# A hybrid attention layer whose planner is given new tasks: scores and products of a block in one task, weights prepared over nineteen superblocks

## The chip, the cores and the metric

The kernel runs on one core of a Trainium2 chip. The metric is device time in microseconds (us) from start to end of the program. Names of engines: PE is TensorE (matmuls), PEld its weight loads, DVE is VectorE, ACT is ScalarE, POOL is GpSimd, SP is SyncE, which issues most of the transfers.

## What is computed

The reference is one layer of an encoder on two requests (4096 and 2048 tokens of width 1024) with shared weights. Cut to what matters:

```python
hn = rms_norm(x, norm_g); proj = hn @ w_in          # 1024 -> 3072 columns, cut into ten pieces
# A: attention over an 8x16 neighbourhood in a 64-wide token grid, 6 heads
s = q . k + bias + mask;  p = softmax(s);  o = p @ v          (per block of 16 columns, 32 key columns)
ya = neighbourhood(qa, ka, va) * silu(na_g)
# B: windowed attention, blocks of 128 tokens see themselves and both neighbours, 6 q heads, 2 kv heads, sink
yb = windowed(qb, kb, vb, sink) * silu(wg)
# C: attention into 256 memory tokens, 4 heads
yc = memory(qc, km, vm) * silu(mg)
y = concat([ya, yb, yc]) @ w_out;  return x + y
```

Every matmul of the kernel is done with operands split into a high and a low fp16 part, as three products (high x high, high x low, low x high) that are summed in PSUM.

## The kernel before

The tokens are cut into 24 **superblocks** of 256 tokens (16 of one request, 8 of the other), each of two blocks of 128. The program has two **stages**. Stage one does, for each superblock: the x tile is loaded, normed and transposed on PE (`xT`, L527), projected to q, k and v of the neighbourhood heads (L302 to L305, one `proj` task is 24 matmuls of 384 columns), q and k are transposed on PE (L730), the gate is projected (`gaten`, L770 to L772, three tasks of 24 matmuls), and then the neighbourhood attention itself is done. Stage two does the windowed and the memory attention and the output projection (token projection L302 to L305 with 448 columns, gate L1217 to L1219, window scores L1268, window products L1320, memory scores L1348, memory products L1411, output L1491 to L1493).

The neighbourhood attention of a superblock takes three pairs of heads `hp`; for each the four column blocks are taken in two pairs `ab` (`PAIRS = ((1, 2), (0, 3))`). One `qk` task (L930) is one `hp` and one `ab`: 12 matmuls of a 64 x 64 tile into two PSUM banks, one for each head. DVE takes a bank into SBUF with bias and running maximum (L947), ACT does the exponential (L957), ACT and DVE split the result in two fp16 parts (L983, L992), two DMA transposes put it in `pt` (L1003), and a `pv` task (L1019, 24 matmuls inside a request, 16 at its ends) makes the products. The window's `wqk` task is one block and two heads (6 matmuls, two banks, six tasks in a superblock), the memory's `mqk` one block (12 matmuls, two banks), `mpv` one pair of heads.

The eight PSUM banks are slots that tasks hold: `SLOTS = {"pj": [0, 1], "sc": [2, 3, 4, 5], "po": [6, 7]}`. The four `sc` slots serve the scores of all three attentions and, in stage one, the transposes of x and of q and k.

**What sets the order.** No engine's order is written out. Each task is added to a `Plan` with an engine, a duration, a priority, the tasks it depends on and the slots it takes and frees (`acq`, `rel`). `Plan.run` plays the tasks through with these durations: an engine that is free takes the ready task of the lowest priority number whose slots are free, and its instructions are written down at that point. So a duration or a priority in the plan costs nothing on the chip itself, but it moves the static order of each engine. On the chip each engine runs its list in order and waits where a semaphore says so.

**The preparation of stage two's weights.** 24 pieces (8 row blocks of three weight matrices) are each loaded twice while stage one runs: a first pass for the maxima (load L812, DVE), a second for the split (load L812, ACT L844, DVE L849, two stores L858). Their priorities are spread by `step`, whose numerator is `NSB - 12.0`, with NSB = 24. SP issues these loads in one queue with the DMA transposes of the neighbourhood attention.

**The border of the stages.** `w1`, one tile of four parts, holds stage one's split weights (a, b, v and the gate n). When its last reader is done, `f_W` makes `w2` in its place (token weights and a part of the gate's), and the loads `wload` (L1114) follow. `f_T3` closes the pools of stage one and holds one `sc` slot for it.

Of the kernel before, what the change touches and what calls it, by code (L numbers as in the profile page):

```python
# [17 lines left out]
P = 128  # L18
D = 1024
NK = 8  # L20
# [35 lines left out]

class Plan:
# [11 lines left out]
    def add(self, eng, dur, fn, deps=(), prio=0.0, lat=None, acq=(), rel=(), label="", slack=0.0, xf=0.0):  # L69
# [4 lines left out]
        t.dur, t.fn, t.prio = dur, fn, prio + SHIFT.get(label, 0.0)  # L74
# [120 lines left out]
def build(tc, A, out, seqs):  # L195
# [190 lines left out]
    w1 = pools["WS"].tile([P, 4, 2, NK, 384], F16, tag="w", name="w1", bufs=1)  # L386
# [4 lines left out]
    W1 = {"a": w1[:, 0], "b": w1[:, 1], "v": w1[:, 2], "n": w1[:, 3], "m": wm}  # L391
# [246 lines left out]
    for gs_ in range(NSB):  # L638
# [125 lines left out]
        for c in range(3):  # L764
# [8 lines left out]
            prg = gs_ + 0.7 + 0.07 * c  # L773
# [6 lines left out]
            t_t = pl.add("act", 0.45, f_t, [t_g, t_TA, t_hgn], prio=prg - 2, acq=["sgn"], label="tanh")  # L780
# [5 lines left out]
            sgn_done[gs_, c] = pl.add("dve", 0.36, f_sg, [t_t], prio=prg - 2, rel=[("pj", "n", gs_, c)], label="sg")  # L786
        pl.add("free", 0.0, lambda: None, xT_use + last_g, rel=["xT"], label="f")
        w_last = xT_use + last_g
# [11 lines left out]
    step = max(NSB - 12.0, 0.5) / (2 * len(pieces))  # L800
# [72 lines left out]
    for gs_ in range(NSB):  # L873
# [25 lines left out]
        for hp in range(3):  # L899
            t_pvs = []  # L900
            for ab in range(2):
                t_pts = []
# [3 lines left out]
                t_es = []  # L906
                pru = prn + (hp * 4 + ab * 2) / 12.0
# [25 lines left out]
                t_s = pl.add("pe", (3 * nk / 2.4 + 200) / 1000, f_s, base, prio=pru, acq=[("sc", u) for u in us], label="qk")  # L933
                last_qk.append(t_s)
# [73 lines left out]
                def f_pv(gs_=gs_, hp=hp, ab=ab, kgs=kgs, edge=edge):  # L1008
# [14 lines left out]
                t_pv = pl.add("pe", 0.82 * len(kgs) / 3, f_pv, t_pTs + (vdep if ab == 0 else []) + t_pvs[-1:],  # L1023
                              prio=pru, acq=[("po", gs_, hp)] if ab == 0 else [], rel=["pt"], label="pv", slack=0)
                t_pvs.append(t_pv)
                last_pv.append(t_pv)
# [58 lines left out]
    def f_T3():  # L1085

        pl.held["pj", "T3"] = pl.held.pop(("sc", "T3"))
        p_close("YN")
        p_close("YA")
        p_open("YB", "left")  # L1090
        for k in ("wo0", "wo1"):
            one("YB", k, [P, NK, D], F16)
        one("YB", "wtab", [P, 6, 384], F32)
    t_T3 = pl.add("free", 0.0, f_T3, ya_use + [t_TC], acq=[("sc", "T3")], rel=[("pj", "T3")], label="T3")

    def f_W():
        w = pools["WS"].tile([P, 24576], F16, tag="w", name="w2", bufs=1)
        for k, o, n, m in (("wt0", 0, NK, 896), ("wt1", 7168, NK, 896), ("wgb", 18432, 9, 640)):
            st[k] = w[:, o:o + n * m].rearrange("p (k c) -> p k c", k=n)
# [9 lines left out]
    def wload(key, src, dep, pr, n, parts=((0, 4), (4, 8)), o=0, slack=0.0):  # L1109

        ts = []
        for k0, k1 in parts:
            def f(k0=k0, k1=k1):
                SY.dma_start(out=st[key][:, k0 - o:k1 - o, :], in_=src[:, k0:k1, :])  # L1114
            ts.append(pl.add("sp", 0.1, f, [dep], prio=pr, label="w2l", xf=n * (k1 - k0) * 256 / 359e3, slack=slack))
        return ts
    t_wt = wload("wt0", w2_d["t"][0], t_W, Q0 - 3.0, 896) + wload("wt1", w2_d["t"][1], t_W, Q0 - 2.99, 896)
    sg_, so_ = 19.7, 15.0
    t_wg = wload("wgb", w2_d["g"][0], t_W, Q0 - 0.5, 640, slack=sg_) + wload(
        "wgb", w2_d["g"][1], t_W, Q0 - 0.49, 640, ((0, 1),), -8, slack=sg_) + wload(  # L1120
# [113 lines left out]

    for nb in range(NB):
# [3 lines left out]
        kbs = [k for k, ok in ((nb - 1, b > 0), (nb, True), (nb + 1, b < 2 * n - 1)) if ok]  # L1239
# [6 lines left out]
        for jh in range(6):  # L1246
# [4 lines left out]
            if kv == 0:  # L1251
                us = [(nb, j), (nb, 3 + j)]

                def f_s(us=us, kbs=kbs, nb=nb, j=j):

                    runs = []
                    for k in kbs:
                        sl = k % NR2
                        if runs and runs[-1][0] + runs[-1][1] == sl:
                            runs[-1][1] += 1  # L1260
                        else:
                            runs.append([sl, 1])
                    o = 0
                    for r0, nr in runs:
                        for pi, (qv, kk) in enumerate(((0, 0), (0, 1), (1, 0))):
                            for v in range(2):
                                prt = slice(64 * v, 64 * v + 64)
                                T.matmul(bank("sc", "w", us[v])[:, o:o + nr * P], st["qT", nb][prt, 5 * qv + j, :],  # L1268
                                         st["ring2"][prt, kk, r0 * P:(r0 + nr) * P], start=(pi == 0), stop=(pi == 2))
                        o += nr * P  # L1270
                t_s = pl.add("pe", (3 * nk / 2.4 + 220) / 1000, f_s, [k_done[k] for k in kbs] + [q2_done[nb], t_T3], prio=pru,
                             acq=[("sc", "w", u_) for u_ in us], label="wqk")
# [8 lines left out]
            t_t = pl.add("dve", 0.12 + nk * 1.04e-3, f_t, [t_s, t_tab2, t_nsk], prio=pru, acq=["pf2"], rel=[("sc", "w", u)], label="wttr")  # L1281
# [5 lines left out]
            t_e = pl.add("act", 0.46 + nk / 1200, f_e, [t_t], prio=pru, label="wexp")  # L1287
# [10 lines left out]
            t_h = pl.add("dve", 0.13 + nk * 0.53e-3, f_h, [t_r], prio=pru, acq=["phl2"], label="whi")  # L1298
# [302 lines left out]
```

## Time and profile before

| what | value |
|---|---|
| time of the runs, median of 3 | 2679.45 us (2678.18 to 2680.52) |
| the profiled execution: time / span in the trace | 2671.06 us / 2669.0 us |
| PE busy | 2576.2 us, 97% of the span |
| DVE / ACT / POOL busy | 71% / 47% / 20% |
| mean granted TensorE clock | 0.987 |

The page reads so: the first section gives for each engine the time in which it was busy; the second cuts the span in 40 slices of 66.7 us and gives in each the busy share in tenths. A matmul's record lasts longer than the time until the next one starts, since they are pipelined: what a matmul costs is read from start to start.

### The profile page before, as it was taken

How to read it: one execution, taken by the hardware profiler on the slowest of the kernel's cores; microseconds unless marked ns; L12 is line 12 of the kernel's file. 1: busy time of each engine (PE TensorE's matmuls, PEld its weight loads, DVE VectorE, ACT ScalarE, POOL GpSimd, SP SyncE). 2: the span in 40 equal slices, each digit the busy share in tenths (PEclk: the TensorE clock that was granted, in tenths of full speed). 3: DMA queues.
4: the chain of work that ended last, by engine and by line, in shares of the span. 5: the costliest groups of instructions: out<-in, count | busy, mean ns of one | idle time of the engine just before them, and what ended most of it. 6: DMA issues, size and time to landing. Idle time of an engine off the chain costs nothing.

```text
span 2669.0 us, 58144 instructions
## 1 busy us (share of the span) xinstructions
PE 2576.2 (97%) x22056; PEld 1573.0 (59%) x22056; DVE 1886.3 (71%) x5283; ACT 1265.8 (47%) x3553; POOL 528.4 (20%) x690
## 2 busy tenths in 40 slices
PE   6999889999999999899999999999999999999999
PEld 3666656666666666655455555555555555555555
DVE  6476776677676666657987777777777767777775
ACT  7465555666565666544343334334333333333332
POOL 2552223323324433230000000011000100000000
PEclk9999999999999999999999999999999999999999
DMA  5485787668577867697665555555555646565554
GB/s 194 151 179 140 182 194 174 163 163 195 145 171 154 209 154 201 156 194 181 144 140 121 117 133 131 123 120 126 123 121 121 125 109 134 130 132 123 117 116 104
DMA packets 728632, 394.54 MB, mean 148 GB/s; under 512 B 645344, under 2 KB 680960, under 8 KB 727712
## 3 DMA queue, kind: packets, MB, share of 16 engines
q1 hardware_dynamic: 714784, 346.59, 58.7%
q0 software_dynamic: 13568, 44.25, 4.7%
q8 instruction: 172, 2.82, 0.4%
q14 instruction: 108, 0.88, 0.1%
HBM read 153.72 MB, written 80.74 MB: 88 GB/s over the span
## 4 chain that ended last, share of the span: by engine, by line
PE 54%; DVE 3%; DMA 1%; POOL 1%; ACT 0%; issue 0%; SPq 0%; ACTq 0%; DVEq 0%; POOLq 0%
PE bank L1491 6%; PE bank L1492 6%; PE bank L1493 6%; PE bank L302 6%; PE bank L303 5%; PE bank L305 5%; PE bank L1217 4%; PE bank L1219 4%; PE bank L1218 4%; PE bank L1268 3%; PE bank L1320 3%; PE bank L1411 1%; PE bank L1348 1%; POOL r L311 1%; DMA w<-w2dt 0%; DVE phl L1302 0%
## 5 line engine op out<-in xcount | busy, mean ns | idle before, releaser
L302 PE MATMUL bank<-w,xT 128*128 128x384 f16 x1152 | 383.4, 334 | 3.3 <-DVE sc_trow L348 1.9
L303 PE MATMUL bank<-w,xT 128*128 128x384 f16 x1152 | 382.1, 333 | 1.2 <-DVE w L364 1.2
L1285 ACT ACTIVATE pf<-pf,sm 128x384 f32<-128x384 f32 (+1 forms) x288 | 173.0, 601 | 345.6 <-DVE sm L1279 344.5
L1491 PE MATMUL bank<-wo,yT 128*128 128x512 f16 x768 | 291.8, 380 | 0.0
L1492 PE MATMUL bank<-wo,yT 128*128 128x512 f16 x768 | 291.1, 379 | 0.0
L1493 PE MATMUL bank<-wo,yT 128*128 128x512 f16 x768 | 291.1, 379 | 0.0
L309 POOL TENSOR_TENSOR r<-r,wA 128x12 f32<-128x12 f32 x48 | 16.1, 336 | 1288.7 <-DVE r L1170 1260.7
L311 POOL TENSOR_TENSOR r<-r,mhalf 128x12 f32<-128x12 f32 (+1 forms) x100 | 224.9, 2249 | 7.8
L305 PE MATMUL bank<-w,xT 128*128 128x384 f16 x1152 | 210.9, 326 | 0.0
L1279 DVE CUSTOM_DVE_ANT_0 pf<-bank,wtab,nsink 128x384 f32<-128x384 f32 (+1 forms) x288 | 165.3, 600 | 57.9 <-PE bank L1268 57.9
L957 ACT ACTIVATE pf<-pf,sm 128x288 f32<-128x288 f32 (+3 forms) x288 | 156.5, 544 | 81.7 <-DVE sm L947 79.4
L992 DVE SCALAR_TENSOR_TENSOR phl<-pf,sm,phl 128x288 f16<-128x288 f32 (+3 forms) x288 | 151.8, 554 | 47.2 <-ACT phl L983 46.2
L1302 DVE SCALAR_TENSOR_TENSOR phl<-pf,sm,phl 128x384 f16<-128x384 f32 (+1 forms) x288 | 174.5, 606 | 9.1
L983 ACT ACTIVATE phl<-pf,sm 128x288 f16<-128x288 f32 (+3 forms) x288 | 146.7, 544 | 45.0 <-ACT pf L957 21.0
L302 PEld LDWEIGHTS <-xT 128*128 128x128 f16 x1152 | 115.1, 100 | 84.9 <-issue 17.7
L770 PE MATMUL bank<-xT,w 128*128 128x256 f16 x576 | 159.0, 276 | 0.2 <-DVE sc_orow L348 0.2
L771 PE MATMUL bank<-xT,w 128*128 128x256 f16 x576 | 158.6, 275 | 0.0
L303 PEld LDWEIGHTS <-xT 128*128 128x128 f16 x1152 | 114.7, 100 | 74.5 <-issue 9.7
L772 PE MATMUL bank<-xT,w 128*128 128x256 f16 x576 | 158.4, 275 | 0.0
L1297 DVE TENSOR_SCALAR phl<-pf,sm 128x384 f16<-128x384 f32 (+1 forms) x288 | 119.1, 414 | 55.2 <-DMA pt<-phl 37.4
L305 PEld LDWEIGHTS <-xT 128*128 128x128 f16 x1152 | 112.8, 98 | 74.8 <-issue 0.3
L1370 ACT ACTIVATE pf<-bank,smm 128x256 f32<-128x256 f32 x192 | 88.9, 471 | 128.6 <-DVE smm L1364 126.9
(279 smaller groups left out, 6044.9 us busy)
## 6 DMA issues: line engine op xcount, KB each, us to landing
xTd<-xT POOLq DMA_DIRECT2D x48, 512.0 KB, 4.3
out<-xr SPq DMA_DIRECT2D x48, 512.0 KB
xx<-in_x_prompt SPq DMA_DIRECT2D x32, 512.0 KB
xr<-in_x_prompt SPq DMA_DIRECT2D x32, 512.0 KB
x<-xTd SPq DMA_DIRECT2D x24, 512.0 KB
w<-xTd SPq DMA_DIRECT2D x24, 512.0 KB
vd<-vhl POOLq DMA_DIRECT2D x48, 192.0 KB, 3.0
va<-vd SPq DMA_DIRECT2D x48, 192.0 KB
```

Of the source, the lines that this page charges most:

```text
L302: T.matmul(ps, xt[:, kk], wh[:, kk, cols], start=(kk == 0), stop=False)
L303: T.matmul(ps, xt[:, kk], wl[:, kk, cols], start=False, stop=False)
L305: T.matmul(ps, xt[:, NK + kk], wh[:, kk, cols], start=False, stop=(kk == NK - 1))
L311: G.tensor_tensor(out=r, in0=r, in1=mhalf[:, 0:n], op=ALU.pow)
L770: T.matmul(pv, wh, x[:, :, kk, :], start=(kk == 0), stop=False)
L771: T.matmul(pv, wh, x[:, :, NK + kk, :], start=False, stop=False)
L1279: V.tensor_tensor_reduce(out=pf[:, 0:nk], in0=bank("sc", "w", u)[:, 0:nk], in1=st["wtab"][:, h, c0:c0 + nk], scale=-1.0, scalar=nsink[:, h ...
L1285: S.activation(out=pf[:, 0:nk], in_=pf[:, 0:nk], func=AF.Exp, scale=-1.0, bias=sm[:, 0:1], accum_out=sm[:, 1:2])
L1302: V.scalar_tensor_tensor(out=phl[:, nk:2 * nk], in0=st["pfw", u][:, 0:nk], scalar=st["smw", u][:, 3:4], in1=phl[:, 0:nk], op0=ALU.mult, op ...
L1491: T.matmul(ps, yT[:, 0, ts_], st["wo0"][:, c, cs], start=(ci == 0), stop=False)
L1492: T.matmul(ps, yT[:, 0, ts_], st["wo1"][:, c, cs], start=False, stop=False)
L1493: T.matmul(ps, yT[:, 1, ts_], st["wo0"][:, c, cs], start=False, stop=(ci == 7))
```

## The change

It has these parts.

1. **Neighbourhood.** The two `qk` tasks of a pair of heads become one, with 24 matmuls, that takes all four `sc` slots; the two `pv` tasks become one with 48 matmuls that waits for the transposes of both pairs of column blocks and frees two `pt` buffers at its end.
2. **Window.** The six `wqk` tasks of a superblock become three, each with two of the six units (block, pair of heads), four slots; the code is now above the loop over blocks (`win_scores`).
3. **Memory.** The two `mqk` tasks of a superblock become one (four slots); the two `mpv` tasks become one, into two halves of one `po` bank.
4. **Preparation.** `step` goes from `NSB - 12.0` to `NSB - 5.0`: 19 in the place of 12.
5. **The border.** The gate's weights n get a tile of their own (`wn`), so that `w2` follows the last v projection, and the part of stage two's gate weights (`wgb`) the last gate n. `f_T3` holds no slot. The gate tasks of the last two superblocks get a priority 1.0 later. The plan's rate for `wload` goes from 359 to 250 (thousand bytes per us), and a delay (`sg_`) is dropped.
6. **Durations in the plan.** A table `TIMES` overrides the duration of twenty kinds of tasks, almost all of stage two; four formulas of the window's tasks get other constants.

```diff
+TIMES = {"tanh": 0.4, "sg": 0.37, "ev": 0.95, "vl2": 0.235, "red2": 0.9, "r8": 2.85, "nrm2": 1.15, "hi2": 0.89, "lo2": 1.0,
...
-        t.dur, t.fn, t.prio = dur, fn, prio + SHIFT.get(label, 0.0)
+        t.dur, t.fn, t.prio = TIMES.get(label, dur), fn, prio + SHIFT.get(label, 0.0)
...
-    w1 = pools["WS"].tile([P, 4, 2, NK, 384], F16, tag="w", name="w1", bufs=1)
+    w1 = pools["WS"].tile([P, 3, 2, NK, 384], F16, tag="w", name="w1", bufs=1)
+    wn = pools["WS"].tile([P, 2, NK, 384], F16, tag="wn", name="wn", bufs=1)
...
-            prg = gs_ + 0.7 + 0.07 * c
+            prg = gs_ + 0.7 + 0.07 * c + (0.0, 1.0)[gs_ >= NSB - 2]
...
-    step = max(NSB - 12.0, 0.5) / (2 * len(pieces))
+    step = max(NSB - 5.0, 0.5) / (2 * len(pieces))
...
-                t_s = pl.add("pe", (3 * nk / 2.4 + 200) / 1000, f_s, base, prio=pru, acq=[("sc", u) for u in us], label="qk")
-                last_qk.append(t_s)
+                f_ss.append((f_s, nk))
+            t_s = pl.add("pe", sum(3 * nk / 2.4 + 110 for _, nk in f_ss) / 1000, lambda f_ss=f_ss: [f() for f, _ in f_ss], base,
+                         prio=prn + hp / 3.0, acq=[("sc", (gs_, 2 * hp + j, ab)) for ab in range(2) for j in range(2)], label="qk")
+            last_qk.append(t_s)
...
-                t_pv = pl.add("pe", 0.82 * len(kgs) / 3, f_pv, t_pTs + (vdep if ab == 0 else []) + t_pvs[-1:],
-                              prio=pru, acq=[("po", gs_, hp)] if ab == 0 else [], rel=["pt"], label="pv", slack=0)
+            t_pv = pl.add("pe", 1.5 * len(kgs) / 3, lambda f_pvs=f_pvs: [f() for f in f_pvs], pv_deps + vdep,
+                          prio=pru, acq=[("po", gs_, hp)], rel=["pt", "pt"], label="pv")
...
-    t_T3 = pl.add("free", 0.0, f_T3, ya_use + [t_TC], acq=[("sc", "T3")], rel=[("pj", "T3")], label="T3")
+    t_T3 = pl.add("free", 0.0, f_T3, ya_use + [t_TC], label="T3")
...
+    def f_Wn():
+        st["wgb"] = pools["WS"].tile([P, 6144], F16, tag="wn", name="wn2", bufs=1)[:, 0:5760].rearrange("p (k c) -> p k c", k=9)
+    t_Wn = pl.add("free", 0.0, f_Wn, wn_last + prep_done, label="Wn")
...
+        units = [(2 * gs_ + blk, j) for blk in range(2) for j in range(3)]
+        for i in range(3):
+            us = units[2 * i:2 * i + 2]
...
+            t_s = pl.add("pe", sum(3 * len(win_keys(nb)) * P / 2.4 + 80 for nb, _ in us) / 1000, f_s,
...
+                         prio=prw, acq=[("sc", "w", (nb, j + 3 * v)) for nb, j in us for v in range(2)], label="wqk")
...
-            t_s = pl.add("pe", 0.85, f_s, [q2_done[2 * gs_ + blk], t_mk, t_T3], prio=prm + blk / 2.0, acq=[("sc", "m", u) for u in us],
-                         label="mqk")
+        t_s = pl.add("pe", 1.45, f_s, [q2_done[2 * gs_], q2_done[2 * gs_ + 1], t_mk, t_T3], prio=prm,
+                     acq=[("sc", "m", (gs_, hp, blk)) for blk in range(2) for hp in range(2)], label="mqk")
...
-            t_pv = pl.add("pe", 0.82, f_pv, t_pts, prio=prm + hp / 2 + 0.25, acq=[("po", "m", gs_, hp)], rel=["ptm"], label="mpv")
+        t_pv = pl.add("pe", 1.4, f_pv, t_mpts, prio=prm + 0.5, acq=[("po", "m", gs_)], rel=["ptm", "ptm"], label="mpv")
```

What this does to the order of the engines is shown at three places, word for word; a name of a tile ends in the number of its buffer or bank.

PE in the middle of stage two, before: the end of a task of window scores (L1268, two banks) and the output projection (L1491) right behind it.

```order
L1268 LDWEIGHTS qT2_23649
L1268 MATMUL bank5_68<-ring2_16691,qT2_23649 128x384
L1268 LDWEIGHTS qT2_23649
L1268 MATMUL bank2_65<-ring2_16691,qT2_23649 128x384
L1491 LDWEIGHTS yT_22858
L1491 MATMUL bank1_64<-wo0_17780,yT_22858 128x512
```

The same place in the changed kernel, where the first unit of a task ends (window scores are L1273 there):

```order
L1273 LDWEIGHTS qT2_23634
L1273 MATMUL bank3_66<-ring2_16991,qT2_23634 128x384
L1273 LDWEIGHTS qT2_23634
L1273 MATMUL bank2_65<-ring2_16991,qT2_23634 128x384
L1273 LDWEIGHTS qT2_23634
L1273 MATMUL bank4_67<-ring2_16991,qT2_23634 128x384
```

Where a full-size matmul followed the two banks of scores, the scores of two more banks now follow.

DVE in stage two, before: the maxima of the memory scores (L1364), the window's result times its gate (L1465), then the rest of the memory softmax.

```order
L1302 SCALAR_TENSOR_TENSOR phl_25419<-pf_25366,sm_25367,phl_25419 128x384
L1364 TENSOR_REDUCE smm<-bank_68 128x2
L1364 TENSOR_REDUCE smm<-bank_65 128x2
L1465 SCALAR_TENSOR_TENSOR sg<-bank_69,sg 128x128 x3
L1376 TENSOR_SCALAR smm<-smm 128x2
```

And in the changed kernel (the maxima are L1400, L1547 is the last step of an output):

```order
L1547 SCALAR_TENSOR_TENSOR xr<-bank_63,oc,xr 128x512
L1400 TENSOR_REDUCE smm<-bank_66 128x2
L1400 TENSOR_REDUCE smm<-bank_65 128x2
L1400 TENSOR_REDUCE smm<-bank_67 128x2
L1400 TENSOR_REDUCE smm<-bank_68 128x2
L1412 TENSOR_SCALAR smm<-smm 128x2
```

Four maxima in a row, of four banks, stand where two stood.

SP's queue in the second part of the first pass of the preparation, before: loads of weights (L812), DMA transposes of the neighbourhood (L1003), loads of x (L500).

```order
L812 DMA xx<-in_w_out 128x1024
L1003 DMA_TRANSPOSE pt<-phl_1240 128x6x128
L500 DMA xx<-in_x_prompt 128x1024
L1003 DMA_TRANSPOSE pt<-phl_1239 128x6x128
L812 DMA xx<-in_w_out 128x1024
L1003 DMA_TRANSPOSE pt<-phl_1240 128x6x128
L1003 DMA_TRANSPOSE pt<-phl_1241 128x6x128
L812 DMA xx<-in_w_out 128x1024
```

And after (L821, L1018, L507):

```order
L821 DMA xx<-in_w_out 128x1024
L1018 DMA_TRANSPOSE pt<-phl_1242 128x6x128
L1018 DMA_TRANSPOSE pt<-phl_1241 128x6x128
L1018 DMA_TRANSPOSE pt<-phl_1242 128x6x128
L821 DMA xx<-in_w_out 128x1024
L804 DMA va<-vd_128 96x1x768
L804 DMA va<-vd_128 128x1x768 x2
L804 DMA va<-vd_128 96x1x768
L507 DMA xx<-in_x_prompt 128x1024
L1018 DMA_TRANSPOSE pt<-phl_1240 128x6x128
```

The loads of `w_out` stand further apart. Counted by the neighbourhood's transposes (12 in a superblock), the 24 loads of the first pass stand at superblocks 3.0 to 5.5 before and 3.1 to 7.3 after; the stores of the second pass end at 20.3 before and 22.4 after.

## Rows read from the trace of the kernel before

**Rows 1.** The page, sections 1 and 2.

```profile
PE 2576.2 (97%) x22056; PEld 1573.0 (59%) x22056; DVE 1886.3 (71%) x5283; ACT 1265.8 (47%) x3553; POOL 528.4 (20%) x690
...
PE   6999889999999999899999999999999999999999
```

**Rows 2.** Busy time of each engine by stretch: us, then PE, PEld, DVE, ACT, POOL, PEclk.

```profile
267.00:467.00 200.00, 179.30 (x1978) 122.02 (x1975) 142.62 (x379) 106.36 (x267) 55.32 (x76) 0.94 0.81 183
467.00:1068.00 601.00, 583.16 (x6580) 398.30 (x6575) 414.19 (x1070) 376.69 (x946) 203.99 (x283) 0.99 0.71 173
1068.00:1334.00 266.00, 246.84 (x2201) 147.60 (x2200) 190.59 (x577) 126.39 (x385) 47.34 (x56) 0.96 0.74 168
1334.00:2602.00 1268.00, 1268.00 (x8878) 713.38 (x8876) 938.25 (x2727) 481.35 (x1542) 113.78 (x120) 1.00 0.58 124
```

**Rows 3.** PE's timeline at window scores: start us, us, line, tiles, shape, count.

```profile
1503.21 0.27 PE L1218 MATMUL bank<-w 128*128 128x256 f16 x1
1503.32 0.27 PE L1219 MATMUL bank<-w,wgc 128*128 128x256 f16 x1
1503.53 0.66 PE L1268 MATMUL bank<-ring,qT 64*128 64x384 f16 x6
1504.12 0.39 PE L1491 MATMUL bank<-wo,yT 128*128 128x512 f16 x1
```

**Rows 4.** PE's timeline, neighbourhood products: one task, then two tasks in one run.

```profile
566.68 0.72 PE L1019 MATMUL bank<-pt,va 128*64 128x128 f16 x24
567.33 0.34 PE L302 MATMUL bank<-w,xT 128*128 128x384 f16 x1
...
749.59 1.24 PE L1019 MATMUL bank<-pt,va 128*64 128x128 f16 x48
750.77 0.56 PE L930 MATMUL bank<-ring,qT 64*64 64x288 f16 x12
```

**Rows 5.** What PE waited for from 267 to 467 us.

```profile
PE bank L1019 <- DMA pt<-phl: 14.5, 8, 4.0
```

**Rows 6.** What SP's queue waited for from 267 to 400 us.

```profile
SPq L812 <- DMA xx<-in_w_in: 24.3, 9, 7.9
SPq L812 <- DMA xx<-in_w_out: 11.4, 6, 4.5
```

**Rows 7.** What PE waited for from 1068 to 1334 us.

```profile
PE bank L930 <- DVE sm L947: 4.9, 8, 1.5
PE bank L1219 <- DMA wgc<-w2dg: 2.8, 2, 2.4
PE bank L1268 <- DVE sm L1279: 2.8, 4, 1.4
PE bank L1348 <- DVE sm L1279: 2.5, 1, 2.5
PE bank L303 <- DMA w<-w2dt: 2.4, 1, 2.4
```

**Rows 8.** The chain that ended last, its longest piece near the border of the stages.

```profile
1122.82 12.34 DMA w<-w2dt
```

**Rows 9.** Timeline around memory scores: PE, the two maxima, the four exponentials.

```profile
1583.27 0.83 PE L1348 MATMUL bank<-mkv,qT 64*128 64x256 f16 x12
...
1585.60 1.28 DVE L1364 TENSOR_REDUCE smm<-bank 128x2 f32<-128x512 f32 x2
1586.38 0.47 ACT L1370 ACTIVATE pf<-bank,smm 128x256 f32<-128x256 f32 x1 [2.53 <-DVE smm L1364]
...
1588.10 0.21 ACT L1370 ACTIVATION_READ_ACCUMULATOR pf<-bank,smm 128x1 f32 x1
```

**Rows 10.** Groups by line and shape: count | busy us, mean ns.

```profile
L947 DVE CUSTOM_DVE_ANT_0 pf<-bank,bA 128x352 f32<-128x352 f32 x120 | 61.9, 516 | 1.2 <-PE bank L930 1.1
L947 DVE CUSTOM_DVE_ANT_0 pf<-bank,bB 128x288 f32<-128x288 f32 x120 | 53.5, 448 | 1.7 <-PE bank L930 1.5
L947 DVE DVE_READ_ACCUMULATOR2_ANT sm<- 128x1 f32 x288 | 23.5, 81 | 0.0
```

**Rows 11.** PE's timeline: transposes, neighbourhood scores, and the next scores one projection later.

```profile
577.72 0.49 PE L730 MATMUL bank<-ident,raw 128*128 128x128 f32 x3
578.14 0.64 PE L930 MATMUL bank<-ring,qT 64*64 64x352 f16 x12
578.72 0.34 PE L302 MATMUL bank<-w,xT 128*128 128x384 f16 x1
...
582.72 0.56 PE L930 MATMUL bank<-ring,qT 64*64 64x288 f16 x12
```

**Rows 12.** An output projection on PE: its first two matmuls.

```profile
1504.35 0.38 PE L1492 MATMUL bank<-wo,yT 128*128 128x512 f16 x1
1504.56 0.38 PE L1493 MATMUL bank<-wo,yT 128*128 128x512 f16 x1
```

More of the change, by code (lines that the diff above doesn't have):

```diff
@@ L779, in f_t @@
                              func=AF.Tanh, scale=hgn)
[L780 removed]
+            t_t = pl.add("act", 0.45, f_t, [t_g, t_TA, t_hgn], prio=prg - 2, acq=["sgn"], label="tanhn")
             def f_sg(gs_=gs_, c=c):
@@ L932, in f_s @@
                         ko += nr * kw
-                t_s = pl.add("pe", (3 * nk / 2.4 + 200) / 1000, f_s, base, prio=pru, acq=[("sc", u) for u in us], label="qk")
-                last_qk.append(t_s)
+                f_ss.append((f_s, nk))
+            t_s = pl.add("pe", sum(3 * nk / 2.4 + 110 for _, nk in f_ss) / 1000, lambda f_ss=f_ss: [f() for f, _ in f_ss], base,
+                         prio=prn + hp / 3.0, acq=[("sc", (gs_, 2 * hp + j, ab)) for ab in range(2) for j in range(2)], label="qk")
+            last_qk.append(t_s)
+            for ab in range(2):
+                t_pts = []
+                kw = CB_KW[PAIRS[ab][0]]
+                nk = (8 if edge else (11 if ab == 0 else 12)) * kw
+                t_es = []
+                pru = prn + (hp * 4 + ab * 2) / 12.0
                 for h in (2 * hp, 2 * hp + 1):
@@ L1232, in build, with win_keys, win_scores, f_s @@
         pl.add("free", 0.0, lambda: None, last_g + [t_prev], rel=["x2"], label="f")
+    def win_keys(nb):
+        b, n = 2 * sbs[nb // 2][1] + nb % 2, sbs[nb // 2][2]
+        return [k for k, ok in ((nb - 1, b > 0), (nb, True), (nb + 1, b < 2 * n - 1)) if ok]
+    def win_scores(nb, j):
+        runs = []
+        for k in win_keys(nb):
+            sl = k % NR2
+            if runs and runs[-1][0] + runs[-1][1] == sl:
+                runs[-1][1] += 1
+            else:
+                runs.append([sl, 1])
+        o = 0
+        for r0, nr in runs:
+            for pi, (qv, kk) in enumerate(((0, 0), (0, 1), (1, 0))):
+                for v in range(2):
+                    prt = slice(64 * v, 64 * v + 64)
+                    T.matmul(bank("sc", "w", (nb, j + 3 * v))[:, o:o + nr * P], st["qT", nb][prt, 5 * qv + j, :],
+                             st["ring2"][prt, kk, r0 * P:(r0 + nr) * P], start=(pi == 0), stop=(pi == 2))
+            o += nr * P
+    t_wqk = {}
+    for gs_ in range(NSB):
+        units = [(2 * gs_ + blk, j) for blk in range(2) for j in range(3)]
+        for i in range(3):
+            us = units[2 * i:2 * i + 2]
+            def f_s(us=us):
+                for nb, j in us:
+                    win_scores(nb, j)
+            nbs = sorted({nb for nb, _ in us})
+            prw = Q0 + gs_ + 1.0 + 0.34 * i - (-0.2 if gs_ == NSB - 1 else 0.0)
+            t_s = pl.add("pe", sum(3 * len(win_keys(nb)) * P / 2.4 + 80 for nb, _ in us) / 1000, f_s,
+                         [k_done[k] for k in sorted({k for nb in nbs for k in win_keys(nb)})] + [q2_done[nb] for nb in nbs] + [t_T3],
+                         prio=prw, acq=[("sc", "w", (nb, j + 3 * v)) for nb, j in us for v in range(2)], label="wqk")
+            for u_ in us:
+                t_wqk[u_] = t_s
     for nb in range(NB):
@@ L1238, in build @@
         b = 2 * g + nb % 2
-        kbs = [k for k, ok in ((nb - 1, b > 0), (nb, True), (nb + 1, b < 2 * n - 1)) if ok]
+        kbs = win_keys(nb)
         c0 = 0 if b > 0 else P
@@ L1251, in build @@
             if kv == 0:
[L1252 to L1272, printed above, removed]
+                t_s = t_wqk[nb, j]
                 win_qk[nb].append(t_s)
@@ L1337, in build, with f_s @@
             t_mk = pl.add("sp", 0.1, f_mk, [t_T2, mkv_st[s]], prio=Q0 + gs_ - 0.6, xf=1.82, acq=["mkv"], label="mk")
-        t_sb = []
-        for blk in range(2):
-            us = [(gs_, hp, blk) for hp in range(2)]
-            def f_s(us=us, s=s, gs_=gs_, blk=blk):
+        def f_s(s=s, gs_=gs_):
+            for blk in range(2):
                 for j in range(2):
@@ L1402, in build, with f_pv @@
                                     rel=["phl2"], label="mpT", xf=0.9))
-            def f_pv(gs_=gs_, hp=hp, s=s):
-                po = bank("po", "m", gs_, hp)[:, 0:256]
+            t_mpts += t_pts
+        def f_pv(gs_=gs_, s=s):
+            for hp in range(2):
+                po = bank("po", "m", gs_)[:, 256 * hp:256 * hp + 256]
                 pt = st["ptm", gs_, hp]
```

58 lines of the change are left out of this document (31 added, 27 removed).

## The prediction

> **What bounds the kernel now.** I read the page first: PE is busy for 97% of the span, and from the twentieth slice on every slice but the last shows a 9 [rows 1]. The busy times by stretch say where the rest is [rows 2]. From 1334 to 2602 us, all but the ends of stage two, PE is busy for 1268.00 of 1268.00 us at a granted clock of 1.00: there nothing but PE's own stream sets the time. In stage one PE is idle for 20.7 of the 200 us from 267 to 467, 17.8 of the 601 us from 467 to 1068, and 19.2 of the 266 us at the border of the stages (1068 to 1334). A busy PE isn't PE at its peak, so the third view is the timeline of PE from start to start. Full-size matmuls of 256 columns follow each other every 0.11 us; where window scores come next, 0.21 us pass, 0.10 more [rows 3]. The six score matmuls run as three pairs, 3 x 384 columns at 2.4 GHz = 0.48 us, but the next full-size matmul starts 0.59 us after the first of them, 0.11 more [rows 3]. So **each change of the tile shape costs PE about 0.10 us**, in which it counts as busy. Products of the neighbourhood tell the same: one task alone takes 0.65 us to the next start, two in one run take 1.18, not 1.30 [rows 4]. The transposes use the full 128*128 shape and count as full size [rows 11].
>
> **What the change removes.** The merged tasks do the same matmuls with fewer changes of shape. I counted them in the static order of PE of both kernels, a change being a step between the full size, the scores' shape and the products' shape. Before there are 919: 425 up to the last neighbourhood product and 494 behind it. After there are 561: 263 and 298. The runs behind it: neighbourhood scores 117 to 71, its products 129 to 71, window scores 144 to 72, memory scores 48 to 24, memory products 47 to 24. 358 changes x 0.10 us = **36 us off PE's stream**: 16 us in stage one (162 changes), 20 us in stage two (196). In stage two PE hides nothing behind others, so all of it is on the path. In stage one PE is idle for 3% of the long middle stretch [rows 2], so most of it is.
>
> **What it adds: tasks that want all four score banks.** Each merged score task (72 of the neighbourhood, 72 of the window, 24 of the memory, 168 in all) can only start when DVE, or ACT for the memory, has left all four. Behind it on PE stands everything else, since PE runs its list in order. Neighbourhood: to empty four banks DVE needs 2 x (0.516 + 0.081) + 2 x (0.448 + 0.081) = 2.25 us [rows 10], and one projection between two such tasks covers 582.72 - 578.72 = 4.0 us [rows 11]; 1.7 us of room while DVE is busy for 69% of the time (414.19 of 601) [rows 2]. Memory: in the new order one output projection (24 x 0.21 = 5.0 us, from [rows 12]) and the products (about 1.2 us) stand between the memory scores and the next window scores. The four maxima and eight exponentials take 0.78 us to the first exponential and 2 x 1.93 us from there, 4.6 us [rows 9]; room 1.6 us, and in the old order DVE came to the maxima 1.5 us after the scores' end [rows 9]. Window: at least a gate and two output projections, over 12 us, follow it before the next score task, for four maxima of the kind of [rows 10]; covered. No wait of this kind is in the trace of stage two, so I bound it: 0 if the room holds, and 72 x 0.61 = 44 us if each neighbourhood task waits as the eight back-to-back ones did at the border (4.9 us in 8) [rows 7]. I take 8 us, near the lower end, since one projection lies between nearly all of them.
>
> **Preparation over nineteen superblocks.** The stretch from 267 to 467 us is the burst of the first pass. PE waited there for `pt` transposes, 14.5 us in 8 waits [rows 5], while SP's queue, which issues these, stood 24.3 + 11.4 us before preparation loads [rows 6]. The clock was 0.94 there: with levels 2.4 and 1.2 GHz that is 12% of 200 us at the lower one, 12 us of work lost. Idle and clock together cost 33 us. The new step does less than its name: the first loads still wait for the same superblock, and 16 of the 24 are as dense as before (superblocks 3.1 to 4.9); only the last eight spread, to 7.3. A third of the burst is my value, **-10 us**, with 0 and -20 as ends. The second pass has the same 24 pieces, later.
>
> **The border of the stages** costs 19.2 us idle and, at a clock of 0.96, half of 8% of 266 us, 30 us together [rows 2]. Its waits have many causes [rows 7]. The gate's weights load a superblock earlier in SP's order, so 2.8 us for `wgc<-w2dg` can go; the gate tasks of the last two superblocks are there as filler. Against it, the preparation ends two superblocks later, and the token weights, whose loads were on the chain for 12.34 us [rows 8], come two rows of SP's queue behind the last store. I take **-4 us**; ends -15 and +12.
>
> The new durations and the loader's rate issue nothing; they act through the order, which is counted above. The new tile `wn` holds the same bytes. The merged `pv` holds two `pt` buffers until its end; four are there, so SP's next transposes find two free.
>
> **Sum.** -36 + 8 - 10 - 4 = -42 us. The profiled execution took 2671.06 us (span 2669.0, 2 us around it), 8 us under the median of the runs; I take the difference off the median: 2679.45 - 42 = **2638 us**, with its own range from 2628 to 2652.
>
> **Rivals.**
> *The waits go too.* The burst gives 20 us and the border 10, the banks cost nothing: -66, 2613 us. For it: both stretches are far from busy. Against it: the first 16 loads are as dense as before.
> *Stage one gives nothing.* Its tasks wait for banks and transposes as long as they saved (16 us), and burst and border stay: only stage two's 20 us are left, 2660 us. For it: in stage one PE waits now and then everywhere, so what it is late for can simply come due.
> *Four-bank lock: slower.* Waits at merged score tasks in stage one also pull the clock down. In the burst 20.7 us of idle time went with 12 us lost to the clock, 0.58 us for each us [rows 2]. If all 72 neighbourhood tasks wait 0.61 us as in [rows 7], that is 44 us and 25 us of clock, 69 in the place of my 8: 2638 + 61 = 2699 us. It turns the result when waits exceed (42 + 8) / 1.58 = 32 us, 0.44 us for each of the 72. Against it: the room of 1.7 us above. The Trainium skill has a rule that speaks for it: its page "TensorE: Matmul & The Clock Gate", section "A second HAM failure mode: psum-queue depth-cycling", says that a PE which idles briefly between groups of matmuls, as it cycles through PSUM banks, makes its clock swing between the two levels; by that rule stage two, at 1.00 now, would lose its clock as well. The trace agrees for stage one's burst (0.94 where PE waits) and shows no case in stage two.
> *No difference.* Half of it: the border loses 12 us, stage one gives nothing, and some memory tasks wait: about 2676 us.
>
> **How the numbers follow.** Forecast 0.42, waits go too 0.20, stage one gives nothing 0.22, no difference 0.07, four-bank lock 0.09. Faster by over 0.2% (5.4 us, about what a measurement of this kernel can tell from no change), that is under 2674: 0.84; within: 0.07; slower: 0.09. The range takes in the first three cases and leaves the last two out, 0.16, and a little of the lower tail: 2612 to 2668.
>
> **What would show it.** Right: in the middle of stage two PE busy without a gap and a superblock's period shorter by 0.8 us (196 / 24 x 0.10); runs of 12 window, 24 memory and 24 or more neighbourhood score matmuls with one step of 0.10 us at either end; PE's waits for L947's and L1279's successors small. The burst's wait for `pt` under 14.5 us and its clock above 0.94. Wrong: waits of PE's score lines for DVE or ACT that come to tens of us, a clock under 1.00 in stage two, or a wait of over 10 us for `w<-w2dt` at the border.

## The result, and the profile of the changed kernel

The changed kernel takes 2634.29 us (median of 4 runs, 2632.43 to 2637.2), the kernel before beside it 2678.81: a ratio of 0.984 [0.9818, 0.9862]. The forecast was 2638, in a range from 2612 to 2668. Three later comparisons, on other occasions, had the kernel before at 2671.4 to 2672.1, near its profiled execution (2671.06), and the changed kernel once more at 2634.37, 0.9852 [0.9837, 0.9867]. So the gain is 37 us by the medians of that comparison and 44 by the first ones; in ratios, 40 and 43 us, give or take 4 to 6. The forecast of 42 can't be told from either. The sum hides more than it shows: what stage one was to give up to the border came out twice as large, and the border's term had the wrong sign.

The page of the changed kernel, sections 1 and 2 (before: [rows 1]):

```profile
span 2633.8 us, 58229 instructions
...
PE 2533.7 (96%) x22056; PEld 1589.7 (60%) x22056; DVE 1884.5 (72%) x5283; ACT 1246.5 (47%) x3553; POOL 520.7 (20%) x690
...
PE   5999999999999999697999999999999999999999
PEclk8999999999999999898999999999999999999999
```

PE does the same 22056 matmuls and is busy for 42.5 us less, while the span is only 35.2 us shorter: PE idles 7 us more than before. Where, its digits tell: a 6 and a 7 in slices 17 and 19, at the border of the stages, where [rows 1] has an 8 and a 9.

Busy time by stretch, same columns and cuts as [rows 2] (its last one shorter, to 2570):

```profile
267.00:467.00 200.00, 186.20 (x2156) 130.03 (x2155) 143.99 (x366) 111.91 (x290) 57.37 (x82) 0.96 0.77 177
467.00:1068.00 601.00, 588.39 (x6780) 411.27 (x6779) 434.23 (x1124) 375.21 (x959) 211.84 (x290) 1.00 0.78 174
1068.00:1334.00 266.00, 228.15 (x1911) 137.50 (x1909) 190.68 (x587) 118.39 (x374) 33.28 (x41) 0.91 0.75 181
1334.00:2570.00 1236.00, 1236.00 (x8792) 719.69 (x8790) 916.83 (x2673) 466.80 (x1518) 110.31 (x120) 1.00 0.59 126
```

Idle time goes from 20.7 to 13.8 us in the burst of the first pass and from 17.8 to 12.6 in the middle of stage one, both at a higher granted clock than in [rows 2]. **At the border it doubles, from 19.2 to 37.8, and the clock falls from 0.96 to 0.91.** Stage two stays without a gap, at 1.00.

Equal cuts in time hold unequal work, so I also read progress at equal work: the columns of PE's matmuls summed in order of start, and the time at which a kernel has reached a sum, less the time of before. The sums of all the kernels in this table are equal at the end. Each is one profiled execution, and not always one near the median of its runs: that of a_step12 took 2635.58 us, 8.3 more than its median, that of b_na_merge 2651.2, 6.6 more, that of a_step16 2623.26, 3.6 less. Us, minus is ahead; the labels are those of the experiments below:

```
where before stands at      450 us   1012    1102    1207    1305    2603
after                       -16.9   -37.2   -38.1   -25.3   -14.0   -35.0
a_again (same kernel)       -17.3   -34.2   -35.2   -24.2   -13.1   -34.2
a_step12                    -12.6   -26.8   -24.1   -27.3   -13.9   -35.0
a_step16                    -12.5   -32.6   -38.7   -38.0   -26.3   -47.3
a_na_split                  -14.1   -16.3   -15.1   -22.7    -8.4   -29.4
b_step19                    -13.1   -13.7    -8.8    -9.0    -9.5    -9.1
b_na_merge                  -13.3   -28.4   -27.4   -21.3   -19.6   -20.0
```

The changed kernel comes to the border **38 us ahead, leaves it 14 us ahead**, and makes another 21 in stage two. The border swallows 24.

What PE waited for there, from 1068 to 1334 us (engine and line, the releaser: us in all, times, longest; before: [rows 7]):

```profile
PE bank L309 <- DMA w<-w2dt: 8.1, 1, 8.1
PE bank L937 <- DVE sm L962: 7.0, 3, 4.4
PE bank L1034 <- DMA pt<-phl: 3.6, 1, 3.6
PE bank L1384 <- DVE sm L1318: 3.4, 2, 2.5
PE bank L308 <- DMA w<-w2dt: 3.0, 1, 3.0
```

First stands the token weights' load, 11.1 us in two waits, against 2.4 in [rows 7]: the sign that the prediction had named for its own border term being wrong. The chain of waits shows what leads there, and its end is the longest piece of the stretch, as in [rows 8]:

```profile
1074.42 9.19 DMA xx<-in_w_out
1083.64 1.16 ACT xhl L853
1084.82 1.28 DVE xhl L858
...
1098.47 1.20 DVE xhl L858
...
1104.72 13.14 DMA w<-w2dt
```

That is the preparation: a piece's load and its split, at 1098.47 the split of the last piece, and at the end the loads of the prepared token weights. In between, from 1086 to 1098 us, the chain runs over DVE, PE and ACT through neighbourhood scores and gates (left out here). SP's queue there (start, us, line, operation, count) has the last stores (L867) and then those loads (L1133):

```profile
1099.10 1.00 SPq L867 DMA_DIRECT2D w2do<-xhl  x2
1102.41 1.10 SPq L1133 DMA_DIRECT2D w<-w2dt  x2
1104.72 0.92 SPq L1133 DMA_DIRECT2D w<-w2dt  x2
```

In before, the last stores, the last gate matmul that reads `w1`, and the loads:

```profile
1053.58 1.00 SPq L858 DMA_DIRECT2D w2do<-xhl  x2
1120.20 0.27 PE L772 MATMUL bank<-xT,w 128*128 128x256 f16 x1
1121.87 1.96 SPq L1114 DMA_DIRECT2D w<-w2dt  x4
```

There the loads came 1.7 us behind the last reader of `w1`, and the last stores stood 68 us ahead of them. In the changed kernel the gate reads `wn`, and the last reader of `w1` is a projection (L311) that is over at 1060 us:

```profile
1058.75 1.30 PE L311 MATMUL bank<-w,xT 128*128 128x384 f16 x7
```

So `w1` comes free 42 us before the loads, and they now follow the last stores, 3.3 us behind these. As far as these starts tell, what held the loads was the gate, and is now the end of the preparation. They start 19 us sooner than in before (17 in a_again), but PE is 38 us ahead. Its timeline there, idle time in brackets:

```profile
1086.60 0.40 PE L937 MATMUL bank<-ring,qT 64*64 64x288 f16 x1 [4.43 <-DVE sm L962]
...
1088.36 0.42 PE L778 MATMUL bank<-xT,wn 128*128 128x256 f16 x1
1088.58 0.42 PE L779 MATMUL bank<-xT,wn 128*128 128x256 f16 x1
...
1099.51 1.95 PE L1034 MATMUL bank<-pt,va 128*64 128x128 f16 x47 [3.64 <-DMA pt<-phl]
...
1104.97 1.34 PE L937 MATMUL bank<-ring,qT 64*64 64x256 f16 x24 [2.25 <-DVE sm L962]
1109.28 0.53 PE L308 MATMUL bank<-w,x 128*128 128x448 f16 x1 [2.97 <-DMA w<-w2dt]
1117.91 0.53 PE L309 MATMUL bank<-w,x 128*128 128x448 f16 x1 [8.10 <-DMA w<-w2dt]
1118.24 0.58 PE L308 MATMUL bank<-w,x 128*128 128x448 f16 x1
1118.61 0.58 PE L309 MATMUL bank<-w,x 128*128 128x448 f16 x1
...
1125.24 0.35 PE L309 MATMUL bank<-w,x 128*128 128x448 f16 x1
1125.43 0.35 PE L308 MATMUL bank<-w,x 128*128 128x448 f16 x1
```

PE stalls five times by 2 us and more in some 35 us. After stalls the same matmuls step at half the rate: 256 columns every 0.21 us instead of 0.11, 448 columns every 0.37 instead of 0.19. That is the lower level of the clock, 1.2 GHz: part of the stalls is paid for a second time.

### The profile page after: what moved, and what is told of

Read it like the earlier page. It is cut to its first block, busy times and chain, and to the rows that moved or that the text cites. A ratio compares the mean times of both kernels' runs of the same rounds, so it can differ in the third digit from the quotient of the medians.

```text
span 2633.8 us, 58229 instructions
## 1 busy us (share of the span) xinstructions
PE 2533.7 (96%) x22056; PEld 1589.7 (60%) x22056; DVE 1884.5 (72%) x5283; ACT 1246.5 (47%) x3553; POOL 520.7 (20%) x690
## 4 chain that ended last, share of the span: by engine, by line
PE 56%; DMA 2%; DVE 1%; SPq 1%; ACT 0%; issue 0%; POOL 0%; DVEq 0%; ACTq 0%; POOLq 0%
PE bank L1532 6%; PE bank L1534 6%; PE bank L1533 6%; PE bank L308 6%; PE bank L309 6%; PE bank L311 5%; PE bank L1236 4%; PE bank L1237 4%; PE bank L1238 4%; PE bank L1359 3%; PE bank L1273 3%; PE bank L1450 1%; PE bank L1384 1%; DMA xx<-in_w_out 1%; DMA w<-w2dt 0%; DMA pt<-phl 0%
## 5 line engine op out<-in xcount | busy, mean ns | idle before, releaser
L315 POOL TENSOR_TENSOR r<-r,wA 128x12 f32<-128x12 f32 x48 | 10.5, 218 | 1259.9 <-DVE r L1189 1255.3
L311 PE MATMUL bank<-w,xT 128*128 128x384 f16 x1152 | 211.3, 327 | 0.0
L777 PE MATMUL bank<-xT,wn 128*128 128x256 f16 x576 | 158.4, 275 | 0.0
L311 PEld LDWEIGHTS <-xT 128*128 128x128 f16 x1152 | 113.0, 98 | 75.2 <-issue 0.9
L778 PE MATMUL bank<-xT,wn 128*128 128x256 f16 x576 | 158.1, 274 | 0.0
L779 PE MATMUL bank<-xT,wn 128*128 128x256 f16 x576 | 158.0, 274 | 0.0
L1172 ACT ACTIVATE raw<-bank 128x448 f32<-128x448 f32 x96 | 47.1, 491 | 226.2 <-PE bank L311 225.6
L1183 DVE SCALAR_TENSOR_TENSOR vw<-bank,vw 128x128 f16<-128x128 f32 x48 | 14.0, 291 | 193.4 <-ACT vw L1176 193.3
```

The costliest lines, as they stand in the source:

```text
L311: T.matmul(ps, xt[:, NK + kk], wh[:, kk, cols], start=False, stop=(kk == NK - 1))
L777: T.matmul(pv, wh, x[:, :, kk, :], start=(kk == 0), stop=False)
L778: T.matmul(pv, wh, x[:, :, NK + kk, :], start=False, stop=False)
```

## The experiments

Two theories of the border stood against each other in the first four runs. Theory A: the step of nineteen makes it dear, since the preparation ends later, and an earlier end gives that time back. Its rival, theory B: the merged four-bank tasks or the gate tasks put there make it dear. That PE comes sooner was in neither theory. Where an expectation gives the letters another meaning, it says so. The border's other edits (`wn`, the slot of `f_T3`, the loader's rate) have no run of their own. Labels with a_ start from the changed kernel, with b_ from the kernel before. Ratios are to the kernel before in the same comparison.

**a_step12 and a_step16: an earlier end of the preparation.** The edit of a_step12; a_step16 has 8.0 in its place.

```diff
-    step = max(NSB - 5.0, 0.5) / (2 * len(pieces))
+    step = max(NSB - 12.0, 0.5) / (2 * len(pieces))
```

> The changed kernel with the preparation spread as before (12.0 in the place of 5.0 in the step's numerator), all else as changed. Theory A (the late end of the preparation is what made the border of the stages dearer: from 1068 to 1334 us PE idles 37.9 us after and 19.2 before, and the clock is 0.91 instead of 0.96): the last stores move from superblock 22.4 back to about 20, the wait of 8.1 us for w<-w2dt goes, the border costs 20 to 30 us less, the burst of the first pass some 7 us more; about 2618 us. Theory B (the border is dearer because of the merged four-bank tasks or the gate tasks put there): the border stays as it is and only the burst gets worse; about 2642 us.

> The changed kernel with 8.0 in the place of 5.0 in the step's numerator: the preparation over sixteen superblocks. Theory A: the preparation ends about two superblocks earlier than in the changed kernel, so the border is cheap and the burst nearly as thin as in the changed kernel: the best of the three, about 2614 us. Theory B: 2634 to 2640 us.

2627.28 us, 0.984 [0.9819, 0.986], and 2626.84, 0.9831 [0.9813, 0.9848]. Neither can be told from the changed kernel (0.984 and 0.9852); theory A's 2618 and 2614 us, ratios of 0.980 and 0.978, lie outside both intervals. The border of a_step12 with a wait in it, then a wait of a_step16:

```profile
1068.00:1334.00 266.00, 238.15 (x2076) 144.09 (x2075) 198.17 (x606) 123.20 (x390) 38.67 (x46) 0.94 0.81 179
PE bank L1238 <- DMA wgc<-w2dg: 5.5, 1, 5.5
```

```profile
PE bank L309 <- DMA w<-w2dt: 5.6, 1, 5.6
```

The border's idle time does fall, from 37.8 to 27.8 us, and in a_step12 the wait for `w<-w2dt` is gone; a load of gate weights, `wgc<-w2dg`, is waited for instead. From 1102 to 1305 us in the table the border now takes 10 us in a_step12 and 12 in a_step16, not 24. What comes of it differs. a_step12 is 14 us less ahead than the changed kernel at 1102 us and even with it at 1305, in an execution above its median. a_step16 is as far ahead at 1102 (-38.7 against -38.1) and 12 us further at 1305, in one below its median. Theory A was right about the wait and about part of the border. A gain in time isn't shown: by the ratios it is 0 to 6 us, less than the intervals can tell.

**b_step19: the step alone, in the kernel before.**

```diff
-    step = max(NSB - 12.0, 0.5) / (2 * len(pieces))
+    step = max(NSB - 5.0, 0.5) / (2 * len(pieces))
```

> The kernel before with only the step's numerator changed from 12.0 to 5.0. Theory A: the burst gives up to 10 us, the border loses 15 to 25 us: slower than before, about 2688 us. Theory B: the burst's gain alone, about 2669 us.

2660.88 us, 0.996 [0.9945, 0.9974]: 11 us off, as theory B said and not theory A. The first stretch is this kernel's burst, the second its border:

```profile
267.00:467.00 200.00, 188.15 (x2171) 128.28 (x2160) 148.45 (x380) 115.79 (x297) 57.21 (x77) 0.98 0.75 177
1068.00:1334.00 266.00, 242.23 (x2092) 142.59 (x2091) 193.84 (x587) 124.97 (x387) 43.37 (x52) 0.96 0.78 182
```

All of its gain is in the burst: idle 20.7 to 11.8 us, clock 0.94 to 0.98. The late end costs the border 4.6 us idle and no clock when PE isn't faster otherwise. So the step alone doesn't make the border what it is.

**a_na_split and b_na_merge: the neighbourhood's merge taken out, and alone.** The core of the edit of b_na_merge; a_na_split has it the other way round. The maxima, exponentials and transposes stay two per task.

```diff
-                t_s = pl.add("pe", (3 * nk / 2.4 + 200) / 1000, f_s, base, prio=pru, acq=[("sc", u) for u in us], label="qk")
...
+            t_s = pl.add("pe", sum(3 * nk / 2.4 + 110 for _, nk in f_ss) / 1000, lambda f_ss=f_ss: [f() for f, _ in f_ss], base,
...
-                t_pv = pl.add("pe", 0.82 * len(kgs) / 3, f_pv, t_pTs + (vdep if ab == 0 else []) + t_pvs[-1:],
...
+            t_pv = pl.add("pe", 1.5 * len(kgs) / 3, lambda f_pvs=f_pvs: [f() for f in f_pvs], pv_deps + vdep,
```

> The changed kernel with the neighbourhood's scores and products as before: one task for each pair of column blocks. Its order has 728 changes of tile shape, 167 more than the changed kernel, nearly all in stage one. Theory A (each change costs PE 0.10 us and PE sets the time in the middle of stage one): 16 us slower than the changed kernel, about 2650 us. Theory B (stage one is held by waits, its changes cost nothing): 2634 us, or less if the four-bank tasks cost more than they save.

> The kernel before with the merged tasks of the neighbourhood alone: 755 changes of tile shape in the place of 919, 163 of the 164 fewer in stage one. Theory A: 16 us less, about 0.994 of the kernel before. If the merged tasks also make the border dearer by themselves, 0 to 6 us less, about 0.998 to 1.0, and idle time at the border of 30 us or more.

a_na_split takes 2641.2 us, 0.9891 [0.9872, 0.991]: without the merge, 10 to 14 us of the gain are gone (against 0.9852 and 0.984), for 167 more changes of the tile shape. b_na_merge takes 2644.62 us, 0.9902 [0.9882, 0.9922]: alone the merge is worth 27 us (21 to 32 by the interval), for 164 fewer changes, 16 us at the assumed price. Its profiled execution shows 20 us, the 16 and some 4 of waits; no trace shows where its median has the other 7. Its middle and border:

```profile
467.00:1068.00 601.00, 590.86 (x6873) 413.72 (x6870) 427.57 (x1096) 377.40 (x966) 207.95 (x290) 0.99 0.78 173
1068.00:1334.00 266.00, 240.03 (x1967) 139.57 (x1964) 193.58 (x584) 119.45 (x373) 41.15 (x49) 0.94 0.77 178
```

In the middle 10.1 us idle stand for 17.8, in the burst 17.0 for 20.7, and at the border 26.0 for 19.2. In the table it is 28 us ahead at 1012 and 20 at 1305. Merged tasks didn't add the waits that I had feared; they took some away, and lost 8 us at the border.

**a_again, a_extra_full, a_extra_same, a_win_split: the price of a change of the tile shape.** a_again is the changed kernel. The two a_extra kernels put one matmul of 8 columns between the two units of each of the 72 merged window score tasks; its result is overwritten by the scores. In the first it has the full-size shape, which makes 144 more changes; in the second the scores' own 64-row shape, which makes none.

```diff
-                for nb, j in us:
+                for i_, (nb, j) in enumerate(us):
+                    if i_ == 1:
+                        T.matmul(bank("sc", "w", (nb, j))[:, 0:8], st["wt0"][:, 0, 0:P], st["wt0"][:, 0, 0:8], start=True, stop=True)
```

In a_extra_same the last line is another:

```diff
+                        r0 = win_keys(nb)[0] % NR2
+                        T.matmul(bank("sc", "w", (nb, j))[:, 0:8], st["qT", nb][0:64, j, :], st["ring2"][0:64, 0, r0 * P:r0 * P + 8],
+                                 start=True, stop=True)
```

a_win_split puts the window's and the memory's tasks on PE back to what they were: 106 more changes.

```diff
-        for i in range(3):
-            us = units[2 * i:2 * i + 2]
...
+                us = [(nb, j), (nb, 3 + j)]
...
-        t_s = pl.add("pe", 1.45, f_s, [q2_done[2 * gs_], q2_done[2 * gs_ + 1], t_mk, t_T3], prio=prm,
...
+            t_s = pl.add("pe", 0.85, f_s, [q2_done[2 * gs_ + blk], t_mk, t_T3], prio=prm + blk / 2.0, acq=[("sc", "m", u) for u in us],
...
-        t_pv = pl.add("pe", 1.4, f_pv, t_mpts, prio=prm + 0.5, acq=[("po", "m", gs_)], rel=["ptm", "ptm"], label="mpv")
+            t_pv = pl.add("pe", 0.82, f_pv, t_pts, prio=prm + hp / 2 + 0.25, acq=[("po", "m", gs_, hp)], rel=["ptm"], label="mpv")
```

> The changed kernel once more, beside the others on the same chip: 0.984 of the kernel before.

> The changed kernel with one small matmul (8 columns, full 128 x 128 shape) put between the two units of each of the 72 merged window score tasks; the scores that follow write over its result, and nothing else moves. It adds 144 changes of tile shape in stage two, where PE never waits. Theory A (a change costs 0.10 us): 14.4 us for the changes and about 2 us for the matmuls, 16 us slower than the changed kernel. Theory B (what looked like a price of the change is the start or the end of a task, whatever its shape): about 2 us slower.

> The same, but the small matmul has the scores' own shape (64 rows): no change of tile shape is added. Both theories: about 2 us slower than the changed kernel, 72 matmuls of some 0.03 us.

> The changed kernel with the window's and the memory's tasks of PE as before (six score tasks of the window and two of the memory in a superblock, two product tasks of the memory), all else as changed. Its order has 667 changes of tile shape, 106 more than the changed kernel, all in stage two. Theory A: 10.6 us slower than the changed kernel, PE without a gap in stage two. Theory B (two-bank tasks leave DVE and ACT more room, which pays): no slower.

```
a_again        2634.37   0.9852 [0.9837, 0.9867]
a_extra_full   2648.06   0.9904 [0.9889, 0.9918]   +13.7 us
a_extra_same   2634.44   0.9856 [0.9841, 0.9871]    +0.1 us
a_win_split    2644.92   0.989  [0.9873, 0.9906]   +10.6 us
```

72 matmuls in the shape of their neighbours cost nothing to be measured; the same 72 in another shape cost 13.6 us, 0.095 us for each of 144 changes (0.05 to 0.13 by the intervals of the two ratios). a_win_split gives 10.6 / 106 = 0.10. PE's timeline shows both, a_extra_full first:

```profile
1607.19 0.66 PE L1273 MATMUL bank<-ring,qT 64*128 64x384 f16 x6
1607.78 0.18 PE L1287 MATMUL bank<-w 128*128 128x8 f16 x1
1607.90 0.67 PE L1273 MATMUL bank<-ring,qT 64*128 64x256 f16 x12
```

```profile
1605.41 0.66 PE L1273 MATMUL bank<-ring,qT 64*128 64x384 f16 x6
1605.91 0.17 PE L1288 MATMUL bank<-ring,qT 64*128 64x8 f16 x1
1605.91 0.68 PE L1273 MATMUL bank<-ring,qT 64*128 64x256 f16 x12
```

From the first scores to the next unit's 0.71 us pass in the one and 0.50 in the other: two changes, 0.21 us, inside a PE that counts as busy all the while. The Trainium skill says, on its page "TensorEngine Tiling (Array Packing)", Key Properties, that a change of the tiling mode, and not of the tile alone, drains the TensorE. The trace agrees that each change costs time, 0.095 us, which the page doesn't give; on what that time goes no run here shows.

**a_prg0 and a_step16_prg0: the gate tasks of the last two superblocks.** In the changed kernel they come 1.0 later in priority, at the border. In a_prg0 they don't; a_step16_prg0 has the 8.0 of a_step16 too.

```diff
-            prg = gs_ + 0.7 + 0.07 * c + (0.0, 1.0)[gs_ >= NSB - 2]
+            prg = gs_ + 0.7 + 0.07 * c + (0.0, 0.0)[gs_ >= NSB - 2]
```

> The changed kernel with the gate tasks of the last two superblocks at their old priority. At the border of the stages (1068 to 1334 us) the changed kernel idles 37.9 us at a clock of 0.91. Theory C (the gate tasks that were put there hold back the close of stage one): the border gets 10 us or more cheaper, about 2622 us. Theory D (they are useful filler, and the border is dear because the merged neighbourhood tasks and the end of the preparation meet there): no change or some us slower, 2634 to 2640 us.

> Both: the preparation over sixteen superblocks, and the gate tasks at their old priority. Theory C: about 2615 us, the fastest so far. Theory D: 2627 to 2635 us, as with sixteen superblocks alone.

2632.58 us, 0.9856 [0.9837, 0.9875], and 2630.44, 0.9846 [0.9831, 0.9862]: no difference, as theory D said. The border of a_prg0 still idles 34.6 us at 0.92. The shift of the gate tasks is neither the border's cause nor its cure.

**a_notimes: the table of durations left out.** 21 more changes of shape, 2 us.

```diff
-        t.dur, t.fn, t.prio = TIMES.get(label, dur), fn, prio + SHIFT.get(label, 0.0)
+        t.dur, t.fn, t.prio = dur, fn, prio + SHIFT.get(label, 0.0)
```

> The changed kernel without the table of durations in the plan. Its order has 582 changes of tile shape, 21 more, all in stage two: 2 us slower if PE stays without a gap there; more if the order built on the other durations makes PE wait in stage two.

2639.95 us, 0.9879 [0.986, 0.9899]. The interval meets that of a_again; some us seem lost, and where stays open. Stage two has no wait on PE here either.

## Why the prediction came out as it did

**Changes of shape, -36: right.** The price was read as 0.10 us and measured as 0.095 by the two a_extra kernels, which differ in nothing else; a_win_split, whose order moves too, gives 0.10. In stage two, where PE hides nothing, the 196 changes were to give 20 us, and the table shows 21 between 1305 and 2603. Of these 2.0 are waits that before still has there, and counted in the traces 170 of the 196 changes lie in this stretch: 0.11 us each. Two slips of the prediction change nothing: the last slice of PE in [rows 1] shows a 9 too, and 2679.45 - 42 is 2637.

**Waits for four banks, +8: right in the small, and no lock.** Score tasks of the neighbourhood waited 0.6 us in the whole middle of stage one, and 7.0 at the border where three stand close together, against 4.9 in [rows 7]. Transposes wait for the same DVE instead, 4.6 us in the middle (from 467 to 1068 us, changed kernel):

```profile
PE bank L737 <- DVE sm L962: 4.6, 3, 3.9
...
PE bank L937 <- DVE sm L962: 0.6, 1, 0.6
```

Against this other waits went that the prediction left in place, so that this stretch idles less than before. The forecast treated each saved change as 0.10 us and nothing more; b_na_merge is 11 us beyond them by its median (27 - 16), 4 in its profiled execution. Stage two kept its clock at 1.00 for 1236 us without an idle moment. So the rule that the rival "four-bank lock" took from the Trainium skill (page "TensorE: Matmul & The Clock Gate", section "A second HAM failure mode: psum-queue depth-cycling"), which speaks of a PE that idles briefly between groups of matmuls, was not put to the test there.

**The burst, -10: right for the step alone, not beside the merge.** Alone the step gives 11 us (b_step19). In the changed kernel the first 450 us give 17, but without the step they already give 12.6 (a_step12), and the merge alone brings 13.3 there (b_na_merge): the step adds some 4. The wait that the prediction named is the one that the step removes, PE's for `pt` transposes from 267 to 467 us. It is 14.5, 11.0 and 10.5 us with twelve superblocks (before, b_na_merge, a_step12), 3.5 in b_step19, and in the changed kernel:

```profile
PE bank L1034 <- DMA pt<-phl: 2.7, 1, 2.7
```

**The border, -4: this step failed.** PE lost 24 us there. The prediction had both pieces in hand, a preparation that ends two superblocks later and loads of token weights behind its last store, and priced them against a PE that keeps its old pace. But the terms weren't independent: the same changes bring PE to the border 38 us sooner. What counts is PE's lead there less the lead of the loads:

```
               PE's lead   first w<-w2dt issue   loads' lead   PE's lead    PE's waits
               at 1102 us  (before: 1121.87)                   less that    for w<-w2dt
before              0            1121.87              0             0            2.4
after            38.1            1102.41           19.5          18.6           11.1
a_again          35.2            1104.41           17.5          17.7           10.7
a_win_split      37.0            1101.71           20.2          16.8           10.9
a_prg0           38.3            1099.12           22.8          15.5            7.0
a_step16         38.7            1087.35           34.5           4.2            5.6
b_step19          8.8            1115.36            6.5           2.3            6.5
b_na_merge       27.4            1094.77           27.1           0.3            6.5
a_step12         24.1            1082.59           39.3         -15.2            none
a_na_split       15.1            1092.65           29.2         -14.1            none
```

The wait follows the difference, with some scatter: about 11 us where PE is 17 to 19 ahead of the loads, none where it is 14 behind. So most of this wait is accounted for. It is less than half of the 24 us; the rest of the border's loss lies in several waits for DVE and transposes and in the clock at 0.91.

That the terms meet, and that neither alone makes the border dear, the first table shows. From 1102 to 1305 us the border takes nothing with the step alone (b_step19), 8 us with the merge alone (b_na_merge), 7 with all but the merge (a_na_split), 10 and 12 with all but the late end (a_step12, a_step16), and 24 with both, 22 in a_again. The times say it too: the merge alone gives 27 us, the step alone 11, the window's and the memory's tasks 11 (a_win_split), 49 in all, and the changed kernel gave 37. Open stays why the remaining loss falls on a different wait in each kernel.

**The sum.** Stage one up to the border was to give 16 - 8 + 10 = 18 us and gave 38; the changes and the idle time of burst and middle (6.9 and 5.2) make some 28 of them, and the higher clock, 0.96 for 0.94 over 200 us and up to 1.00 for 0.99 over 601, at most another 10. The border was to give 4 and took 24. Stage two gave its 20. 18 + 4 + 20 had to be 42 and was 38 - 24 + 21 = 35 in the profiled executions. That the total came near was luck: two errors, of +20 and -28, nearly cancel. They are linked, since a PE that is early is part of what makes the border dear, but they are not one: a_step16 is as early (38.7) and loses 12 there. The rival "waits go too" held up to 1102 us, "stage one gives nothing" for what was left of it behind the border, 14 of 38.

No variant was shown to beat the changed kernel: a_step16 has the lowest ratio (0.9831), and its interval overlaps those of the changed kernel.

## What to carry to other kernels

Where an engine looks fully busy, look at start-to-start times between instructions of different shape: a fixed step at each change is work that grouping takes away, and a count of the changes times that step is a forecast that held here (0.10 us read, 0.095 measured). Add up terms of a sum only where they don't meet: whatever speeds up one stage brings its end sooner to the loads of the next, so read at equal work, and not at equal time, who is ahead of whom at the border. And a gain in the middle of a stage counts once it is seen behind the border.

## What the hardware showed that I had not expected

A matmul of 8 columns between others of the same tile shape costs nothing that can be measured (72 of them: 0.1 us, where the runs of one kernel differ by several), and in another shape 0.19 us, twice a change. Four-bank tasks in stage two left the clock at 1.00. After the border's stall of 8.1 us 448 columns took 0.37 us instead of 0.19 for some 6 us, so that the stall cost another 3 us.
